# A decoder layer on one core: every engine's order written by hand from the third chunk of the input projection to the end of the attention

## The chip, the cores and the metric

The kernel runs on one core of a Trainium2 chip. Its time is the device time of one execution in microseconds (us); several executions of a kernel are taken, and the median stands for it. The core has five engines that work side by side, each through a queue of its own in a fixed order: PE (TensorE, matrix products), DVE (VectorE), ACT (ScalarE), POOL (GpSimd) and SP (SyncE, which here issues nearly all transfers). An instruction that waits holds up everything behind it in its queue, and nothing else.

## The reference

One layer of a decoder for 256 positions with a model width of 2048, batch 1, all in float32:

```python
a_in = _rmsnorm(h, attn_norm_g[i])
proj = a_in @ w_in[i]
z, xbc, dt_raw, q, k, v = jnp.split(proj, [o1, o2, o3, o4, o5], axis=-1)
xbc = jax.nn.silu(_causal_dwconv(xbc, conv_w[i], conv_b[i]))
xs, bm, cm = jnp.split(xbc, [SSM_INNER, SSM_INNER + SSM_GROUPS * SSM_STATE], axis=-1)
dt = jax.nn.softplus(dt_raw.astype(jnp.float32) + dt_bias[i].astype(jnp.float32))
...
y = y + d_skip[i].astype(jnp.float32)[:, None] * xs_h.astype(jnp.float32)
y = y.reshape(b, s, SSM_INNER) * jax.nn.silu(z.astype(jnp.float32))
...
y_att = _swa_sinks(qh, kh, vh, sinks[i])
h = h + jnp.concatenate([y_ssm, y_att], axis=-1) @ w_out[i]
u = _rmsnorm(h, ffn_norm_g[i]) @ w_up[i]
u = _causal_dwconv(u, ffn_conv_w[i], ffn_conv_b[i])
g_ff, u_ff = jnp.split(u, [D_FF], axis=-1)
h = h + (jax.nn.silu(g_ff) * u_ff) @ w_down[i]
gate = jax.nn.sigmoid(_rmsnorm(h, ple_norm_g[i]) @ w_ple_gate[i])
pe = _rmsnorm(p[i] @ w_ple_proj[i], ple_post_g[i])
h = h + gate * pe
```

The state-space part (SSD) has four groups with 8 heads of 64, a state of 128 and two chunks of 128 positions. The attention has 32 query heads and 8 key and value heads of 64, a window of 128 and a sink for each head; queries and keys are normalised for each head and partly rotated.

## The kernel before

**Steps.** All weights pass through PE in 476 steps of one kind. A step takes 512 KB of weights (`KW = 2` tiles of 128 rows by `NC = 512` columns). SP loads them into `w`; ACT casts them to `wh`, a float rounded to PE's fast format; DVE subtracts, `wl = w - wh`; and PE multiplies twelve times, for 2 row tiles, 2 blocks of 128 positions and three products (high by high, L219; weight's low part, L220; activation's low part, L221). The ring of `w` has `WR = 7` buffers, those of `wh` and `wl` have `WB = 4`. A step's twelve products go to a pair of accumulators, of which there are two pairs; a chunk of `w_in` has 8 steps, a part of `w_out` two for each group of 512 inputs and each 512 outputs.

**Stages.** The first two chunks (B and C of the SSD) and the step sizes `dt` come first. Then follow the 176 steps that the change concerns, counted from 0 at the first step of the third chunk: for each of four groups g a chunk for x and one for z (steps 0 to 63, group g ends its x chunk at 16g + 7), `w_out` of group 0 (64 to 71), the first queries (72 to 79), keys, values, two more chunks of queries (to 111), `w_out` of groups 1 and 2 (112 to 127), the last queries (to 135), `w_out` of 3 and 4 (to 151), and of 5, 6 and 7 (to 175; 4 to 7 are the attention's outputs). Steps 176 to 475 are the feed-forward part and the embedding.

**Beside the steps.** For each group, `ssd_x` scales x out of the accumulators (`scaled`, ACT), turns it to channels, convolves it (`conv_tile`: one ACT operation L266 and three DVE operations L268 for each 128 channels), applies silu, and turns it back. `decays` loads the sums of the step sizes (`seg`), masks them on POOL and takes 16 exponentials on ACT (L513); `decays_cb`, `state` and `heads` are the matrix products of the scan. `norm_rope` normalises and rotates queries and keys, `scores` computes a block of 8 or 4 heads and its softmax, and `values` the product with v. Turning a float32 tile takes three engines: a copy that takes the 16-bit halves apart (`half`), a DMA transpose that SP issues (`flip`), and a copy on POOL that puts them together (`together`, L284). The first copy stands on ACT for x, B, C and y (L293, 128x1024, twenty times) and for the probabilities (L800), otherwise on POOL.

**What sets the order.** In this region only PE's order is the order of the program:

```python
order.enter_context(tc.manual_schedule(engines={PE.engine}))
```

For the other engines a scheduler chooses, by its own model of times. `chunk` and `output` are generators that emit a step at a time, and `plan(n, event)` names the step after which a piece is emitted (decays of a group 4 steps after its x chunk's end, `decays_cb` 9, `state` 18, `heads` 20; scores and values by a table). The feed-forward part is left to the scheduler.

Of the kernel before, what the change touches and what calls it, by code (L numbers as in the profile page):

```python
# [30 lines left out]
WR = 7  # L31
# [34 lines left out]
def hybrid_layer(  # L66
# [208 lines left out]
    def transposed(pool, n, put):  # L275

        half = sb(pool, [P, 2, n], "half", U16)
        put(half)
        flip = sb(pool, [P, 2 * n // P, P], "flip", U16)
        nc.sync.dma_start_transpose(flip, half.rearrange("p a n -> p (a n)"))  # L280
        return flip

    def together(dst, flip):
        G.tensor_copy(dst.bitcast(U16).rearrange("p c (t a) -> p c t a", a=2), flip.rearrange("p (a c) t -> p c t a", a=2))  # L284

    def flipped(pool, dst, n, put):

        together(dst, transposed(pool, n, put))

    def to_channels(pool, t):  # L290

        flips = [
            transposed(pool, NC, lambda half: S.copy(half, halves(t[:, b * NC : (b + 1) * NC]))) for b in range(NB)  # L293
        ]
        for b in range(NB):
            together(v3(t, 4)[:, :, b * P : (b + 1) * P], flips[b])

    def convolve(src, dst, cw, ntap, c0):

        for f in range(4):  # L300
            w = cw[:, (c0 + f) * (ntap + 1) : (c0 + f + 1) * (ntap + 1)]
            conv_tile(src[:, f, :], dst[:, f, :], [w[:, j : j + 1] for j in range(ntap)], w[:, ntap : ntap + 1])

# [58 lines left out]
    def scaled(acc, pool):  # L362

        t = sb(pool, [P, NB * NC], "xa")
        for b in range(NB):
            S.activation(out=t[:, b * NC : (b + 1) * NC], in_=acc[b], func=AF.Copy, scale=rx[:, b : b + 1])
        return t
# [27 lines left out]

    held = {}
    cos_t = sin_t = None
    at = {}
    step = [0]

    def chunk(c, then):
        acc = acc_pair()
        n = KT // KW
        for s in range(n):
            products(acc, aT, load_w(w_in[c, s]), s * KW, KW, KT, s == n - 1)
            if s == n - 1:
                then(acc)
            yield

    def output(*groups):  # L410

        ys_ = [held.pop(i) for i in groups]
        total = KG * len(groups)
        for n in range(4):
            acc = acc_pair()
            for s in range(2 * len(groups)):
                yT = ys_[s // 2]
                products(acc, lambda k, b: yT(k % KG, b), load_w(w_out[groups[s // 2] * 2 + s % 2, n]), s * KW, KW, total, s == 2 * len(groups) - 1)
                if s == 2 * len(groups) - 1:
                    add_to_h(acc, n)  # L420
                yield

    def run(part):
        for _ in part:
            if step[0] in at:
                for event in at[step[0]]:
                    event()
            step[0] += 1

    def plan(n, event):  # L430
        at.setdefault(n, []).append(event)


    order = ctx.enter_context(ExitStack())
    order.enter_context(tc.manual_schedule(engines={PE.engine}))
    with tc.tile_pool(name="ssd", bufs=1) as sp, tc.tile_pool(name="ssd2", bufs=2) as sp2, tc.tile_pool(name="dram", bufs=1, space=bass.MemoryType.DRAM) as dp:
        BT = sb(sp, [P, 4, T], "BT")
        CT = sb(sp, [P, 4, T], "CT")
        raw = [scaled(acc, sp2) for acc in (acc_b, acc_c)]
        for c, (t, dst) in enumerate(zip(raw, (BT, CT))):  # L440
            to_channels(sp2, t)
            convolve(v3(t, 4), dst, scw, 4, 16 + 4 * c)
            S.activation(out=dst, in_=dst, func=AF.Silu)

        dt = sb(sp, [P, 64], "dt")
        dt4 = dt.rearrange("p (g c h) -> p g c h", g=4, c=NB)
        adt = sb(sp, [P, 64], "adt")
        adt4 = adt.rearrange("p (g c h) -> p g c h", g=4, c=NB)
        acs = sb(sp, [P, 64], "acs")
        eacs = sb(sp, [P, 64], "eacs")  # L450
        nacs = sb(sp, [P, 64], "nacs")
        scr = dp.tile([64, P], F32, tag="scr", name="scr")

        def steps_dt():
            tr = tr_tile()
            for b in range(NB):
                PE.matmul(tr[:, b * 32 : (b + 1) * 32], lhsT=dtT[:, b * P : (b + 1) * P], rhs=sel, start=True, stop=True)
            u = sb(sp, [P, 4, NB, 8], "dt_u")
            for b in range(NB):
                V.scalar_tensor_tensor(  # L460
                    out=u[:, :, b, :], in0=v3(tr[:, b * 32 : (b + 1) * 32], 4), scalar=rx[:, b : b + 1], in1=v3(dtb, 4), op0=ALU.mult, op1=ALU.add
                )
            u = u.rearrange("p g c h -> p (g c h)")
            e = sb(sp, [P, 64], "dt_e")
            e1 = sb(sp, [P, 64], "dt_e1")
            l1 = sb(sp, [P, 64], "dt_l1")
            V.scalar_tensor_tensor(out=e, in0=u, scalar=-1.0, in1=u, op0=ALU.mult, op1=ALU.min)
# [543 lines left out]
```

## Time and profile before

| | |
|---|---|
| median of 3 runs | 1451.29 us (1448.86 to 1456.82) |
| the profiled execution, its time | 1453.72 us |
| the profiled execution, its span | 1452.0 us |
| PE's mean granted clock | 0.989 |
| DMA, mean | 207 GB/s, 299.95 MB |

One execution was recorded by the hardware profiler. The page's first part gives each engine's busy time, its share of the span and the number of its instructions. A group of instructions is told by its line, engine and operation, `out<-in`, the shape, the count, the busy time, the mean of one in ns, and the idle time of the engine just before them with what ended it (the releaser). A row of the waits reads: what waited, for what, us in total, times, longest. A row of the timeline has the start, the length, the engine and line, the operation and its count, and in brackets how long the engine was idle before it and what released it. A row on windows has the stretch and its length, each engine's busy time with the number of its instructions, PE's granted clock, DMA's share and its rate.

### The profile page before, as it was taken

The page shows a single profiled execution, that of the slowest core. Times are in us where ns is not written, and L with a number is a line of the kernel's source. Part 1 is how long each engine was busy: PE and PEld are TensorE (multiplying, and loading weights), DVE is VectorE, ACT ScalarE, POOL GpSimd, SP SyncE. Part 2 cuts the span into 40 slices and gives each one's busy share as a digit, 9 for nine tenths or more (in the row PEclk, how much of TensorE's full clock was granted, in tenths as well). Part 3 has the DMA queues.
Part 4 walks back from the last instruction along what each step waited for, and adds up shares of the span by engine and source line. Part 5 has one row for each costly group of instructions (what it writes and reads, how often), then busy time and mean ns, then how long its engine had stood idle before and what let it go on. Part 6 is the DMA issues. An engine that isn't in the chain of part 4 may idle for free.

```text
span 1452.0 us, 17980 instructions
## 1 busy us (share of the span) xinstructions
PE 1421.6 (98%) x6404; PEld 1161.6 (80%) x6404; DVE 979.6 (67%) x1209; ACT 831.1 (57%) x1156; POOL 344.5 (24%) x270
## 2 busy tenths in 40 slices
PE   9999999899899899999999999999999999999998
PEld 6878878788687687888888888888888888888886
DVE  6677758656486878666676746665675576476854
ACT  6785866755465746455565545544553554455643
POOL 0112422405574241001433201411320231120000
PEclk9999999999899999999999999999999999999999
DMA  9867769667587786668878768867876877776671
GB/s 339 267 191 218 220 179 256 171 176 217 145 209 193 199 225 171 208 188 226 223 206 227 205 190 228 211 210 204 211 214 198 219 211 208 206 207 187 213 222 66
DMA packets 193034, 299.95 MB, mean 207 GB/s; under 512 B 122608, under 2 KB 125488, under 8 KB 192560
## 3 DMA queue, kind: packets, MB, share of 16 engines
q1 hardware_dynamic: 192512, 298.33, 72.4%
q8 instruction: 50, 0.82, 0.2%
q10 hardware_dynamic: 432, 0.48, 0.1%
q14 instruction: 40, 0.33, 0.1%
HBM read 268.32 MB, written 2.13 MB: 186 GB/s over the span
## 4 chain that ended last, share of the span: by engine, by line
PE 67%; DVE 0%; issue 0%; ACT 0%; DVEq 0%
PE acc L219 22%; PE acc L220 22%; PE acc L221 22%; PE tr L814 1%; PE tr L252 0%; PE sc L777 0%; DVE sg L941 0%; DVE den L796 0%; DVE wl L193 0%; DVE sg L942 0%; DVE yl L193 0%; DVE h L372 0%; ACT s L792 0%; ACT sg L940 0%; DVEq L1007 0%
## 5 line engine op out<-in xcount | busy, mean ns | idle before, releaser
L193 DVE TENSOR_TENSOR wl<-w,wh 128x1024 fp32r<-128x1024 f32 (+1 forms) x493 | 637.1, 1298 | 412.4 <-ACT wh L192 411.2
L192 ACT CAST wh<-w 128x1024 fp32r<-128x1024 f32 (+1 forms) x493 | 514.4, 1049 | 489.5 <-PE acc L221 460.7
L219 PE MATMUL acc<-wh,ah 128*128 128x512 f32 x1280 | 504.9, 395 | 6.4 <-ACT wh L192 6.4
L220 PE MATMUL acc<-wl,ah 128*128 128x512 f32 x1280 | 501.7, 392 | 5.3 <-DVE wl L193 5.3
L221 PE MATMUL acc<-wh,al 128*128 128x512 f32 x1280 | 501.0, 391 | 0.0
L219 PEld LDWEIGHTS acc<-wh,ah 128*128 128x128 f32 x1280 | 241.9, 189 | 61.3 <-ACT wh L192 7.9
L220 PEld LDWEIGHTS acc<-wl,ah 128*128 128x128 f32 x1280 | 242.0, 189 | 58.5 <-DVE wl L193 6.8
L221 PEld LDWEIGHTS acc<-wh,al 128*128 128x128 f32 x1280 | 242.0, 189 | 50.6
L220 PE MATMUL acc<-wl,gh 128*128 128x512 f32 x352 | 137.0, 389 | 0.0
L221 PE MATMUL acc<-wh,gl 128*128 128x512 f32 x352 | 137.0, 389 | 0.0
L219 PE MATMUL acc<-wh,gh 128*128 128x512 f32 x352 | 136.4, 389 | 0.0
L891 POOL COPY half<-u 128x1024 uint16<-128x1024 uint16 x44 | 60.1, 1376 | 266.0 <-ACT u L889 266.0
L219 PE MATMUL acc<-wh,yh 128*128 128x512 f32 x256 | 102.3, 400 | 5.0 <-ACT z L571 5.0
L220 PE MATMUL acc<-wl,yh 128*128 128x512 f32 x256 | 100.8, 394 | 0.0
L221 PE MATMUL acc<-wh,yl 128*128 128x512 f32 x256 | 100.5, 393 | 0.0
L894 POOL COPY uc<-flip 128x1024 uint16<-128x1024 uint16 x44 | 54.2, 1232 | 175.9 <-DMA flip<-half 175.9
L220 PEld LDWEIGHTS acc<-wl,gh 128*128 128x128 f32 x352 | 66.1, 188 | 13.7
L221 PEld LDWEIGHTS acc<-wh,gl 128*128 128x128 f32 x352 | 66.1, 188 | 13.7
L219 PEld LDWEIGHTS acc<-wh,gh 128*128 128x128 f32 x352 | 66.1, 188 | 13.6
L268 DVE SCALAR_TENSOR_TENSOR cv<-uc,fcw,cv 128x254 f32<-128x254 f32 (+1 forms) x176 | 73.1, 476 | 1.7 <-ACT cv L266 1.7
L219 PEld LDWEIGHTS acc<-wh,yh 128*128 128x128 f32 x256 | 48.6, 190 | 18.5 <-ACT z L571 5.2
L372 DVE TENSOR_TENSOR h<-h,acc 128x512 f32<-128x512 f32 x96 | 62.2, 679 | 1.1 <-PE acc L221 1.1
(227 smaller groups left out, 1194.5 us busy)
## 6 DMA issues: line engine op xcount, KB each, us to landing
w<-in_w_up_dram SPq DMA_DIRECT2D x176, 512.0 KB, 4.2
w<-in_w_in_dram SPq DMA_DIRECT2D x126, 512.0 KB, 4.3
w<-in_w_down_dram SPq DMA_DIRECT2D x88, 512.0 KB, 4.2
w<-in_w_out_dram SPq DMA_DIRECT2D x64, 512.0 KB, 4.4
w<-in_w_pg_dram SPq DMA_DIRECT2D x32, 512.0 KB, 4.2
seg<-scr SPq DMA_DIRECT2D x8, 512.0 KB, 4.9
xt<-in_xT_dram SPq DMA_DIRECT2D x16, 128.0 KB, 6.4
h<-in_x_dram SPq DMA_DIRECT2D x2, 1024.0 KB, 8.5
```

What stands on the lines that cost most here:

```text
L192: S.copy(hi, src)
L193: V.tensor_tensor(out=lo, in0=src, in1=hi.bitcast(F32), op=ALU.subtract)
L219: PE.matmul(acc[b], lhsT=hi, rhs=wh[:, i, :], start=(k == 0), stop=False)
L220: PE.matmul(acc[b], lhsT=hi, rhs=wl[:, i, :], start=False, stop=False)
L221: PE.matmul(acc[b], lhsT=lo, rhs=wh[:, i, :], start=False, stop=(k == total - 1))
L268: V.scalar_tensor_tensor(out=dst[:, s:], in0=ps[:, : T - s], scalar=taps[n - 1 - s], in1=dst[:, s:], op0=ALU.mult, op1=ALU.add)
L372: V.tensor_tensor(out=hs, in0=hs, in1=acc[b], op=ALU.add)
L814: PE.matmul(v3(o[e * HD : (e + 1) * HD, kv * 2 * P : (kv + 1) * 2 * P], 2), lhsT=v[kb][:, vs], rhs=pT[e][:, :, kb, :], start=(kb == 0), st ...
L891: G.tensor_copy(half.rearrange("p (a n) -> p a n", a=2), u_.bitcast(U16).rearrange("p (n a) -> p a n", a=2))
L894: G.tensor_copy(uc[:, :, b * P : (b + 1) * P].bitcast(U16).rearrange("p f (t a) -> p f t a", a=2), flip.rearrange("p (a f) t -> p f t a", ...
```

## The change

From step 0 to step 175 `manual_schedule()` now holds for all engines: every queue has the order of the program. The program is a list of 176 steps, and `run` works through it. In iteration n SP gets the loads up to step n + 8 and ACT the cast of step n + 3 (`ahead`), PE the products of step n, then every chain that is due gets its next piece (`wake`), and last DVE gets the low part of step n + 3 (`low`). A chain is a generator; `yield 5` lets it sleep for five steps. The SSD's `state`, `heads` and the rest of a group are one chain now, `ssd_x`; `add_to_h` is a chain that runs one step after the last product; `rotary`, which computes cosines and sines in some fifty small DVE operations, runs in nine pieces from step 34. The first scores stand two steps later.

Beside the order: `WR` is 6. The twenty copies L293 on ACT are ten copies twice as wide on POOL, and two transposes of 1024 columns are one of 2048. All `half` and `flip` tiles share a pool, `mid`, with two buffers of each; most tiles of the SSD have one buffer instead of two. Table loads on ACT are 17 instead of 22.

```diff
-WR = 7
+WR = 6
...
     def to_channels(pool, t):
-        flips = [
-            transposed(pool, NC, lambda half: S.copy(half, halves(t[:, b * NC : (b + 1) * NC]))) for b in range(NB)
-        ]
+        half = half_tile(pool)
+        G.tensor_copy(half, halves(t))
+        flip = turn(pool, half)
+        yield 5
...
+    def spawn(chain, delay=1):
+        sleepers.setdefault(now[0] + delay, []).append(chain)
+
+    def wake():
+        for chain in sleepers.pop(now[0], []):
+            n = next(chain, 0)
+            if n:
+                spawn(chain, n)
...
+    def ahead(steps):
+        for k in range(len(loaded), min(now[0] + WR + WB - 1, len(steps))):
+            loaded[k] = sb(wp, [P, KW, NC], "w", bufs=WR)
+            nc.sync.dma_start(loaded[k].rearrange("p a b -> p (a b)"), steps[k][0])
+        lows = []
+        for k in range(len(ready), min(now[0] + WB, len(steps))):
+            ready[k] = sb(wp, [P, KW, NC], "wh", F32R), sb(wp, [P, KW, NC], "wl", F32R)
+            S.copy(ready[k][0], loaded[k])
+            lows.append(k)
+        return lows
...
+    def run(steps, until):
+        while now[0] < until:
+            lows = ahead(steps)
+            steps[now[0]][1](ready[now[0]])
+            wake()
+            low(lows)
+            now[0] += 1
...
-    order.enter_context(tc.manual_schedule(engines={PE.engine}))
+    order.enter_context(tc.manual_schedule())
+    mid = mix.enter_context(tc.tile_pool(name="mid", bufs=2))
...
+        yield 1
+        for c in range(NB):
+            for h in range(8):
+                i = heads_[c].start + h
+                S.activation(out=seg[c][:, h, :], in_=seg[c][:, h, :], func=AF.Exp, bias=nacs[:, i : i + 1])
+                if c and h == 3:
+                    yield 1
+            if not c:
+                yield 1
+        yield 2
...
+    low(ahead(steps))
+    scaled(acc_b, raw_b)
+    scaled(acc_c, raw_c)
+    spawn(steps_dt(), 0)
+    spawn(b_or_c(raw_b, BT, 16), 0)
+    spawn(b_or_c(raw_c, CT, 20), 4)
+    spawn(rotary(), 34)
...
             p = s.rearrange("p h w -> p (h w)")
-            flipped(ap_, p.rearrange("p (c t) -> p c t", t=P), 2 * m * W, lambda half: S.copy(half, halves(p)))
+            half = half_tile(mid)
+            S.copy(half, halves(p))
+            flip = turn(mid, half)
+            yield 4
+            together(p.rearrange("p (c t) -> p c t", t=P), flip)
...
-        for j, first, value in ((0, (30, 33, 36), 50), (1, (43, 46, 51), 65), (2, (58, 61, 66), 79), (3, (75, 77, 80), 93)):
+        for j, first, value, wait in ((0, (32, 36, 39), 49, 8), (1, (44, 48, 52), 62, 1), (2, (56, 60, 65), 75, 6), (3, (74, 77, 80), 90, 1)):
```

What this makes of the queues is shown at three places. The first is ACT at the start of the region, before the change: casts of the weights (L192), the scaling of B and C out of the accumulators (L366), and their copies (L293).

```order
L192 CAST wh_632<-w_631 128x1024
L192 CAST wh_650<-w_649 128x1024
L192 CAST wh_668<-w_667 128x1024
L366 ACTIVATE xa_563<-acc_29_147,rx_145 128x512
L366 ACTIVATE xa_563<-acc_30_148,rx_145 128x512
L293 COPY half_569<-xa_563 128x1024
L366 ACTIVATE xa_566<-acc_31_149,rx_145 128x512
L293 COPY half_573<-xa_563 128x1024
```

And ACT at the same place now, where casts are L465 and the scaling is L367.

```order
L465 CAST wh_589<-w_571 128x1024
L465 CAST wh_592<-w_573 128x1024
L465 CAST wh_595<-w_575 128x1024
L465 CAST wh_598<-w_577 128x1024
L367 ACTIVATE xa_563<-acc_29_147,rx_145 128x512
L367 ACTIVATE xa_563<-acc_30_148,rx_145 128x512
L367 ACTIVATE xc_564<-acc_31_149,rx_145 128x512
L367 ACTIVATE xc_564<-acc_32_150,rx_145 128x512
```

The cast of step 3 has come ahead of the scaling, and the copies are gone from ACT.

The second is ACT about step 14, in group 0, before: the exponential of `dec` (L507), the convolution of x (L266), the 16 exponentials of `seg` (L513) and the casts.

```order
L507 ACT_TABLE_LOAD
L507 ACTIVATE dec_949<-dec_949 128x8
L192 CAST wh_1037<-w_1036 128x1024
L266 ACTIVATE xc_810<-xa_797,scw_133 128x256 x4
L513 ACTIVATE seg_947<-seg_947,nacs_627 128x128 x8
L513 ACTIVATE seg_963<-seg_963,nacs_627 128x128 x8
L192 CAST wh_1055<-w_1054 128x1024
L192 CAST wh_1082<-w_1081 128x1024
```

Now the same place (dec at L562, C's silu at L497, `seg` at L571); the casts are those of steps 16, 17, 18 and 19.

```order
L562 ACT_TABLE_LOAD
L562 ACTIVATE dec_928<-dec_928 128x8
L497 ACT_TABLE_LOAD
L497 ACTIVATE CT_562<-CT_562 128x1024
L465 CAST wh_941<-w_807 128x1024
L571 ACT_TABLE_LOAD
L571 ACTIVATE seg_176_872<-seg_176_872,nacs_569 128x128 x8
L465 CAST wh_969<-w_835 128x1024
L266 ACTIVATE xc_984<-xa_826,scw_133 128x256 x2
L571 ACTIVATE seg_177_873<-seg_177_873,nacs_569 128x128 x4
L465 CAST wh_1000<-w_855 128x1024
L266 ACTIVATE xc_984<-xa_826,scw_133 128x256 x2
```

The exponentials stand in three pieces with casts between, and C's silu with its table has come between `dec` and the cast of step 16.

The third is DVE about step 153, where the softmax of two blocks of scores meets `w_out` of the first attention outputs, before: the scores' mask (L781), the maximum (L788), the sums (L796 to L798), the additions to h (L372) and low parts (L193).

```order
L796 TENSOR_TENSOR den_4764<-den_4764,es_4769 128x4
L193 TENSOR_TENSOR yl_1016_4819<-tr_4827,yh_1015_4818 128x4x128
L797 RECIPROCAL den_4764<-den_4764 128x4
L798 TENSOR_TENSOR s_1002_4754<-s_1002_4754,den_4764 128x1024
L193 TENSOR_TENSOR wl_4948<-w_4946,wh_4947 128x1024
L781 TENSOR_TENSOR s_1024_4858<-sc_4859,band_120 128x1024
L372 TENSOR_TENSOR h_1_83<-h_1_83,acc_1019_4838 128x512
L372 TENSOR_TENSOR h_2_84<-h_2_84,acc_1020_4839 128x512
L788 TENSOR_REDUCE nm_4865<-s_1024_4858 128x4
L193 TENSOR_TENSOR wl_4966<-w_4964,wh_4965 128x1024
```

Now (sums L908 to L910, mask L891, maximum L898, the step's low part L471):

```order
L193 TENSOR_TENSOR yl_1011_4837<-tr_4664,yh_1010_4836 128x4x128
L908 TENSOR_TENSOR den_4785<-den_4785,es_4783 128x4
L909 RECIPROCAL den_4785<-den_4785 128x4
L910 TENSOR_TENSOR s_992_4756<-s_992_4756,den_4785 128x1024
L891 TENSOR_TENSOR s_1012_4845<-sc_4811,band_120 128x1024
L898 TENSOR_REDUCE nm_4847<-s_1012_4845 128x4
L471 TENSOR_TENSOR wl_4822<-w_4678,wh_4821 128x1024
L372 TENSOR_TENSOR h_1_83<-h_1_83,acc_1004_4797 128x512
L372 TENSOR_TENSOR h_2_84<-h_2_84,acc_1005_4798 128x512
```

The sums of one block, the mask and the maximum of the next now stand in one piece, and the additions to h behind it and behind the low part.

More of the change, by code (lines that the diff above doesn't have):

```diff
@@ new lines, in hybrid_layer, with chunk, step, products_of @@
+    sleepers = {}
+    now = [0]
+    def spawn(chain, delay=1):
[5 more added lines that the diff above has]
+                spawn(chain, n)
+    def chunk(c, then):
+        n = KT // KW
+        acc = []
+        def step(s):
+            def products_of(w):
+                if s == 0:
+                    acc.extend(acc_pair())
+                products(acc, aT, w, s * KW, KW, KT, s == n - 1)
+                if s == n - 1:
+                    then(acc)
+            return products_of
+        return [(w_in[c, s], step(s)) for s in range(n)]
```

588 lines of the change are left out of this document (312 added, 276 removed).

## The prediction, made before the changed kernel had run

> **What bounds the kernel now.** I read the page first, then the waits of PE, then windows of the span, and last the timeline at the places that the windows point to.
>
> ```profile
> span 1452.0 us, 17980 instructions
> PE 1421.6 (98%) x6404; PEld 1161.6 (80%) x6404; DVE 979.6 (67%) x1209; ACT 831.1 (57%) x1156; POOL 344.5 (24%) x270
> PE sc L777 <- POOL kT L284: 6.7, 1, 6.7
> PE acc L219 <- ACT wh L192: 6.4, 3, 2.4
> PE acc L220 <- DVE wl L193: 5.3, 4, 3.1
> PE acc L219 <- ACT z L571: 5.0, 1, 5.0
> ```
>
> PE is busy for 98% of the span, and nothing here changes its matmuls. So the change can only win PE's waits and what they bring. The last four rows (us in total, times, longest) are nearly all of these waits: 23.4 us. The windows say where they lie (length, then busy time and count for PE, PEld, DVE, ACT and POOL, PE's clock, DMA share, GB/s):
>
> ```profile
> 54.24:625.70 571.46, 548.12 (x2534) 441.83 (x2533) 413.51 (x523) 364.46 (x586) 189.61 (x155) 0.97 0.72 199
> 625.70:1443.00 817.30, 817.30 (x3627) 677.02 (x3626) 526.63 (x586) 428.74 (x519) 152.14 (x103) 1.00 0.73 205
> 700.00:800.00 100.00, 100.00 (x443) 82.81 (x442) 67.08 (x80) 57.69 (x70) 31.78 (x20) 1.00 0.80 218
> 99.33:111.69 12.36, 9.23 (x30) 6.96 (x29) 8.49 (x15) 12.27 (x24) 2.02 (x2) 0.73 0.40 134
> 207.55:218.51 10.96, 7.98 (x30) 6.17 (x29) 3.07 (x4) 10.90 (x19) 3.82 (x4) 0.84 0.28 73
> 262.13:275.73 13.60, 8.60 (x30) 6.80 (x29) 6.74 (x8) 13.12 (x22) 4.98 (x5) 0.75 0.47 111
> 376.38:392.51 16.13, 9.45 (x41) 7.46 (x40) 6.67 (x6) 3.62 (x4) 7.60 (x5) 0.68 0.79 170
> 464.56:481.01 16.45, 10.90 (x38) 7.74 (x36) 10.90 (x12) 13.34 (x19) 7.50 (x4) 0.90 0.68 166
> ```
>
> The first row is the stretch whose order is rewritten, steps 0 to 175; the second is the rest, where PE never waits and runs at full clock. The third gives the price of a step: 443 matmuls in 100 us are 0.226 us each, so a step of twelve takes 2.71 us. The last five rows hold steps 16-17, 49-50, 65-66, 102-103 and 127-129: 11 steps, which at that price are 29.8 us, in 69.5 us. The counts add up to 169, 37 more than the steps' 132; these are 128 columns wide or less where a step's matmuls have 512, for which I allow 0.08 us each, 3 us. So **36.7 us** are lost at five places: about 6.5, 5.0, 7.6, 9.4 and 8.3. Only 23.4 of them are idle; the other 13.3 are work at a lower clock behind the gaps, 0.57 us for each idle one. With all of it gone the profiled execution (1453.7 us) would take 1417.0: the floor of everything below.
>
> ACT is busy for 12.27 of 12.36, 10.90 of 10.96 and 13.12 of 13.60 us in the first three places: there a cast that PE needs stands behind other work on ACT. The fourth is one wait for the turned keys on POOL. The fifth and the first are waits inside an engine's queue:
>
> ```profile
> 464.54 1.90 ACT L800 COPY half<-s 128x2048 uint16<-128x2048 uint16 x1 [8.14 <-DMA flip<-half]
> 95.85 0.21 ACT L507 ACTIVATE dec<-dec 128x8 f32<-128x8 f32 x1 [2.83 <-DVE dec L506]
> 95.97 1.04 ACT L192 CAST wh<-w 128x1024 fp32r<-128x1024 f32 x1
> 96.91 2.07 ACT L266 ACTIVATE xc<-xa,scw 128x256 f32<-128x256 f32 x4
> 98.89 4.78 ACT L513 ACTIVATE seg<-seg,nacs 128x128 f32<-128x128 f32 x16
> 104.65 0.58 PE L219 MATMUL acc<-wh,ah 128*128 128x512 f32 x1 [2.45 <-ACT wh L192]
> 106.51 0.63 PE L221 MATMUL acc<-wh,al 128*128 128x512 f32 x1
> ```
>
> At 464.54 ACT had stood for 8.14 us on a copy that waited for a buffer, with casts behind it. At 95.85 it had waited 2.83 us, and then 2.07 of convolution and 4.78 of exponentials ran ahead of the next casts; PE then stood 2.45 us, and its matmuls took 0.63 us behind it.
>
> **The change, part by part.** *The groups' chains.* The sixteen exponentials now run as 8, cast, 4, cast, 4, and the convolution in pairs of two, so at most 2.4 us (half of 4.78) stand between two casts. A cast starts when PE has left the buffer, three steps ahead: 8.1 us, less 1.04 for itself, are 7.1 us of slack. The twenty ACT copies L293 go to POOL, and table loads fall from 22 to 17. For groups 1 to 3 the pieces of one step (1.04 + 1.04 + 1.2) come to little over a step, so ACT falls behind by less than the slack: steps 49-50 and 65-66 lose nothing, a gain of 12.6. Bounds: 0 to 12.6; I take all, since those windows are full on ACT and it is exactly ACT that is relieved.
>
> *Group 0* has C's silu and its table besides. From `dec` in step 12 to the casts' end in step 13 ACT has 1.5 (table, exponential), 2.3 (table, silu), 1.04 (cast) and 3.7 (table, eight exponentials): 8.5 us in two steps of 5.4, hence 3.1 late. In step 14 a cast and two convolutions add 2.1; then DVE does six additions, and only behind them the low part that PE needs at step 17, 8.1 us after step 14 began.
>
> ```profile
> 95.89 2.14 POOL L508 TENSOR_SCALAR_AFFINE_SELECT seg<-seg 128x1024 f32<-128x1024 f32 x2 [6.05 <-DVE dec L506]
> 97.04 2.08 DVE L193 TENSOR_TENSOR wl<-w,wh 128x1024 fp32r<-128x1024 f32 x1 [1.22 <-ACT wh L192]
> 99.04 4.80 DVE L268 SCALAR_TENSOR_TENSOR xc<-xa,scw,xc 128x255 f32<-128x255 f32 x12
> 104.63 2.36 DVE L193 TENSOR_TENSOR wl<-w,wh 128x1024 fp32r<-128x1024 f32 x2 [0.79 <-ACT wh L192]
> 105.57 1.28 ACT L571 ACT_TABLE_LOAD   x1
> 107.45 1.05 ACT L540 ACTIVATE xc<-xc 128x1024 f32<-128x1024 f32 x1
> ```
>
> 3.1 + 2.1 + 2.4 (half of 4.80) + 1.2 are 8.8, 0.7 too late, and a wait of `dec` for its data as before (2.83) comes on top: 3.5 idle, and 2 to 3 at half clock. That is about what this place loses now, so I keep its **6.5**. Bounds 0 (the data come in time) to 10.
>
> *The start.* Before the first product ACT now makes four casts, not three, ahead of the scaling that frees PE's accumulators.
>
> ```profile
> 50.55 1.05 ACT L192 CAST wh<-w 128x1024 fp32r<-128x1024 f32 x1 [1.67 <-PE acc L338]
> 51.51 1.26 ACT L366 ACTIVATE xa<-acc,rx 128x512 f32<-128x512 f32 x2
> ```
>
> The fourth cast's buffer comes free one step after the third's, at 50.55 + 2.72 = 53.3; cast and first scaling end at 53.3 + 1.05 + 0.63 = 55.0, where PE now starts at 54.24. **+1.0** (0 to 1.5).
>
> *The keys.* Now both key transposes stand late, and PE waits 6.7:
>
> ```profile
> 376.58 5.12 SPq L280 DMA_TRANSPOSE flip<-half  x1
> 382.88 5.05 SPq L280 DMA_TRANSPOSE flip<-half  x1
> 376.70 3.09 POOL L752 COPY half<-qkr 128x1024 uint16<-128x1024 uint16 x2
> 383.77 2.11 POOL L284 COPY kT<-flip 128x2048 uint16<-128x2048 uint16 x1 [3.98 <-DMA flip<-half]
> w<-in_w_in_dram SPq DMA_DIRECT2D x126, 512.0 KB, 4.3
> ```
>
> In the new order the keys' copies stand in steps 91 and 92 and their turning back in 97 and 98; the first scores stand at 104 instead of 102. The chain of copy 3.1, issue 5.1, landing 2.1 (381.70 to 383.77) and copy 2.1 fits twice into twelve steps: the 9.4 go. But both transposes hold up SP's weight loads: a load is issued eight steps ahead of its products, five ahead of its cast, 13.6 us, of which it takes 4.3; 9.3 remain, and two transposes of 5.1 fill 10.2. **+1.0** (0 to 5) at step 101.
>
> *The attention.* A block of probabilities goes to values in 16 steps; from its copy to the values stand five, 13.6 us.
>
> ```profile
> L284 POOL COPY s<-flip 128x2048 uint16<-128x2048 uint16 x12 | 28.4, 2368 | 73.7 <-DMA flip<-half 54.8 <-PE acc L221 18.9
> L781 DVE TENSOR_TENSOR s<-sc,band 128x1024 f32<-128x1024 f32 x12 | 14.6, 1216 | 6.5 <-PE sc L777 6.5
> L788 DVE TENSOR_REDUCE nm<-s 128x4 f32<-128x1024 f32 x8 | 9.7, 1210 | 0.1
> L798 DVE TENSOR_TENSOR s<-s,den 128x1024 f32<-128x1024 f32 x12 | 16.1, 1340 | 0.2
> L372 DVE TENSOR_TENSOR h<-h,acc 128x512 f32<-128x512 f32 x46 | 29.9, 677 | 0.0
> ```
>
> Copy 1.9, issue 5.1, landing 2.1 and turning back 2.4 are 11.5, so ACT and DVE may be 2.1 late. In the steps where two blocks meet DVE has 1.2 (low part) + 1.22 + 1.21 + 1.34, and a carry of additions or a split (1.35): 6.3 in a step of 2.7. I take DVE to be 5 late at the first values (step 121): **+3.0** idle (0 to 7); the later values have longer waits behind them. At output 5 the additions to h now stand one step later, behind such a step: 6.3 + 1.35 against the two steps (5.4) after which PE wants the accumulators, 2.3, and the small ones of the step: **+2.8** (0 to 5). The fifth place (8.3) goes: ACT's copies now stand where their buffers should be free.
>
> *The rest.* One raw weight buffer less takes a step off the loads' lead, everywhere:
>
> ```profile
> L192 ACT CAST wh<-w 128x1024 fp32r<-128x1024 f32 (+1 forms) x493 | 514.4, 1049 | 489.5 <-PE acc L221 460.7
> ```
>
> The casts' idle time ends with PE 460.7 of 489.5 us, not with a load: I cost it at nothing (0 to 3), hidden by loads that wait for buffers. Rotary's small operations on DVE move into steps 34 to 42, between stalls: nothing (0 to 2).
>
> *The clock.* The new gaps, 1.0 + 1.0 + 3.0 + 2.8 = 7.8, bring 0.57 us of slow work each: 4.5 (0 to 7). [...]
>
> **The sum:** 1417.0 + 6.5 + 1.0 + 1.0 + 3.0 + 2.8 + 4.5 = 1435.8 us against the profiled 1453.7, 17.9 less. The median of the runs (1451.29) lies 2.4 below that execution; from it, 17.9 less is 1433.4: I predict **1433.5**.
>
> **The rivals.** *A, nearly all waits go:* the terms of the attention and the keys are zero, the start and half of group 0 remain: 1417.0 + 1.0 + 3.3 + 0.6 = 1422, by the median 1419.5. For it: each of my new terms is a lateness of 0.7 to 3 us against slacks worked out from mean durations.
>
> *B, POOL's new copies hold up DVE:* ten copies 128x2048 at some 2.2 us come to POOL. Above, the low part at 97.04 took 2.08 us beside POOL's work on `seg`; two undisturbed took 2.36. If each copy costs the low part 0.9, and half-clock work follows (0.57), ten are 14: 1435.8 + 14 = 1450, by the median 1447.5. For it: the 2.08. Against: a low part has slack, and 0.9 matters only where it is used up. [...]
>
> *C, slower:* in a fixed order a copy that waits for one of the two buffers stands ahead of the casts, as at 464.54, where one wait of 8.14 cost 8.3. The scores' twelve copies, the queries' and keys' ten and the groups' fourteen now share two `half` and two `flip` buffers. From three such places on, 25 us, the gain is gone by more than 0.5%; with four it is 1435.8 + 33 = 1469, by the median 1466.5. Against: most copies have five steps between, and a chain of 11.5 us fits.
>
> *D, it does nothing that counts:* PE's waits only move to the next piece (group 0 shows how), 1449 to 1454. I count it with B.
>
> **How the numbers follow.** Forecast 0.52 (1427 to 1441), A 0.20 (1417 to 1427), B and D 0.17 (1441 to 1455), C 0.11. The range that leaves out C and A's last few: 1418 to 1453. A measurement of this kernel can tell 0.5%, 7.3 us, from no change: faster than 1444 are the forecast, A and a little of B, 0.73; within, 0.16; slower than 1458.5, 0.11.
>
> **What would show it.** Right: PE's waits on ACT near steps 49 and 65 and on kT absent; a first gap of about 1 us at the first product of the third chunk; a gap of 2 to 5 us at step 17; one of a few us at the first values. Wrong: casts whose idle time ends with a transpose or with a `w` load; PE gaps in 625 to 1443, where there are none now (the seventh buffer); low parts of 2 us in most steps.

## The result and the profile after

The changed kernel takes 1460.58 us (median of 14 runs, 1459.29 to 1465.48); the kernel before took 1452.28 us beside it (14 runs). The ratio is 1.0059 with a 95% interval of 1.0047 to 1.0071: slower by 8.3 us, where 17.9 less had been forecast. The profiled execution took 1459.82 us, 6.1 more than the one profiled before the change; of these 6.1, 4.0 lie in the 176 steps, 1.4 ahead of them and 0.7 behind.

The page's first part of the changed kernel, then its waits of PE (us in total, times, longest):

```profile
span 1458.1 us, 17885 instructions
PE 1420.3 (97%) x6404; PEld 1158.6 (79%) x6404; DVE 1006.5 (69%) x1209; ACT 806.2 (55%) x1131; POOL 365.8 (25%) x276
PE acc L220 <- DVE wl L471: 16.0, 9, 4.1
PE acc L219 <- ACT z L597: 5.3, 1, 5.3
PE tr L932 <- POOL s L284: 4.3, 2, 2.5
PE tr L252 <- DVE h L372: 2.2, 1, 2.2
PE acc L219 <- DVE h L372: 1.7, 1, 1.7
PE acc L219 <- ACT xa L367: 0.8, 1, 0.8
```

The wait for kT is gone and ACT does 25 us less (831.1 before, 806.2 now). But PE's wait for the low parts has gone from 5.3 to 16.0 us in nine places, its wait for z is 5.3 where it was 5.0, and four small waits are new. DVE does the same 1209 instructions in 27 us more. The windows of the rewritten steps and of the rest:

```profile
55.61:631.11 575.50, 545.85 (x2525) 437.61 (x2526) 436.62 (x569) 341.17 (x561) 212.10 (x163) 0.99 0.66 198
631.11:1449.89 818.78, 818.78 (x3637) 678.84 (x3637) 534.70 (x588) 429.76 (x523) 151.13 (x102) 1.00 0.73 205
```

The rest still has no wait (818.78 us against 817.30 in a stretch cut a little otherwise). The rewritten steps take 575.50 instead of 571.46 us, and step 0 starts at 55.61 instead of 54.24. So the question is asked in these 176 steps. For each place I took the time from one step's first matmul to the next step's, less 2.72 us a step and less the other matmuls in it (at what they cost where nothing waits); that is what the place loses, idle time and slow work together. The forecast's terms stand beside it, and the last column is the best of the experiments, e14:

| steps | before | forecast | changed | e14 |
|---|---|---|---|---|
| 0 | 0 | 1.0 | 0.8 | 0.8 |
| 11 to 14 | 0 | 0 | 3.3 | 4.3 |
| 16 to 18 | 6.5 | 6.5 | 6.3 | 0.4 |
| 34 | 0.1 | 0 | 1.7 | 1.7 |
| 37 | 0 | 0 | 5.0 | 0 |
| 49 to 50 | 5.1 | 0 | 3.7 | 1.7 |
| 65 to 66 | 7.7 | 0 | 8.0 | 1.7 |
| 71 to 72 | 0 | 0 | 0.3 | 2.7 |
| 101 to 103 | 9.5 | 1.0 | 0 | 0 |
| 118 to 122 | 0 | 3.0 | 2.3 | 1.9 |
| 127 to 129 | 8.1 | 0 | 0.1 | 0.1 |
| 132 | 0 | 0 | 2.0 | 0 |
| 147 to 148 | 0 | 0 | 4.6 | 0.3 |
| 155 to 158 | 0 | 2.8 | 2.2 | 0.7 |
| 175 | 0 | 0 | 2.3 | 2.3 |
| slow work behind new gaps | | 4.5 | (in the rows) | (in the rows) |
| sum | 37.0 | 18.8 | 42.6 | 18.6 |

The two wins in the attention came as forecast, 17.5 us. They were given back at places where the sum had zeros. The two sums differ by 23.8 us, and the profiled execution missed the forecast for it, 1435.8, by 24.0: the table holds nearly the whole miss.

### The profile page after: what moved, and what is told of

It is laid out like the page before. It is cut to its first block, busy times and chain, and to the rows that moved or that the text cites. A ratio compares the mean times of both kernels' runs of the same rounds, so it can differ in the third digit from the quotient of the medians.

```text
span 1458.1 us, 17885 instructions
## 1 busy us (share of the span) xinstructions
PE 1420.3 (97%) x6404; PEld 1158.6 (79%) x6404; DVE 1006.5 (69%) x1209; ACT 806.2 (55%) x1131; POOL 365.8 (25%) x276
## 4 chain that ended last, share of the span: by engine, by line
PE 80%; DVE 8%; ACT 4%; issue 3%; DMA 2%; POOL 2%; SPq 0%; DVEq 0%; POOLq 0%; ACTq 0%
PE acc L219 25%; PE acc L220 25%; PE acc L221 25%; DVE wl L471 3%; DMA flip<-half 1%; ACT wh L465 1%; PE acc L339 1%; PE acc L340 1%; DVE xc L268 1%; PE acc L338 1%; PE ms L643 1%; ACT seg L571 1%; POOL s L284 1%; DMA seg<-scr 1%; ACT s L906 1%
## 5 line engine op out<-in xcount | busy, mean ns | idle before, releaser
L193 DVE TENSOR_TENSOR wl<-w,wh 128x1024 fp32r<-128x1024 f32 (+1 forms) x317 | 416.7, 1317 | 279.8 <-ACT wh L192 279.2
L192 ACT CAST wh<-w 128x1024 fp32r<-128x1024 f32 (+1 forms) x317 | 332.4, 1048 | 358.1 <-PE acc L221 341.2
L471 DVE TENSOR_TENSOR wl<-w,wh 128x1024 fp32r<-128x1024 f32 x176 | 237.7, 1357 | 90.9 <-ACT wh L465 90.5
L465 ACT CAST wh<-w 128x1024 fp32r<-128x1024 f32 x176 | 182.2, 1047 | 168.2 <-PE acc L221 128.9
```

Source lines behind the costliest of these rows:

```text
L192: S.copy(hi, src)
L193: V.tensor_tensor(out=lo, in0=src, in1=hi.bitcast(F32), op=ALU.subtract)
L465: S.copy(ready[k][0], loaded[k])
L471: V.tensor_tensor(out=ready[k][1], in0=loaded[k], in1=ready[k][0].bitcast(F32), op=ALU.subtract)
```

## The experiments

Four theories went into the runs. **1**: each wait has a piece of its own that stands at a bad place, and the places add up. **2**: POOL's new copies hold up DVE. **3**: weights come late, for want of a buffer or behind wide transposes. **4**: the attention's copies and transposes wait for one of two buffers, of the halves or of the flips. All experiments alter the changed kernel. Medians of before, taken beside each set, were 1454.39 (e1 to e4), 1453.66 (e5 to e8), 1454.95 (e9 to e11), 1453.12 (e12) and 1452.92 us (e13 to e15), and ratios are against these. Since before was up to 2.7 us slower in these sets than beside the changed kernel (1452.28), a gain counted from 1460.58 is uncertain by as much, and the ratios are safer.

Each kernel has one trace, and places that an edit doesn't touch differ between traces too. From the changed kernel to e7, all with two flips, 132 loses 0 to 2.0, 147 to 148 loses 2.8 to 6.6, and step 122 nothing or 1.7. The traced executions of e3, e4 and e7 took 3.0 to 4.2 us more than their medians.

### e1: z of group 3 earlier

```diff
-        steps += chunk(3 + 2 * g, lambda acc, g=g: spawn(ssd_z(g, acc), 3))
+        steps += chunk(3 + 2 * g, lambda acc, g=g: spawn(ssd_z(g, acc), 3 if g < 3 else 1))
```

> The z of group 3 is read out of its accumulators one step after its chunk's end instead of three. Theory 1 (each wait of PE has its own badly placed piece; here z stands two steps behind the step that needs its accumulators): PE's wait of 5.3 us at step 66 goes with the slow work behind it, 5 to 7.6 us less than the changed kernel's 1460.6, so 1453 to 1456. Theory 2 (POOL's new copies hold up DVE's low parts everywhere): the low part of step 66 is late by itself and takes the wait's place, under 2 us less.

Measured: 1457.91 us, ratio 1.0027 (1.0014 to 1.0039). The timeline of the changed kernel shows the wait, ACT first, then PE (start, length, in brackets the idle time before and what ended it):

```profile
272.76 1.04 ACT L465 CAST wh<-w 128x1024 fp32r<-128x1024 f32 x1
275.55 1.28 ACT L609 ACT_TABLE_LOAD   x1 [1.76 <-DVE xc L268]
276.85 1.06 ACT L609 ACTIVATE xc<-xc 128x1024 f32<-128x1024 f32 x1
277.81 1.97 ACT L465 CAST wh<-w 128x1024 fp32r<-128x1024 f32 x2
279.69 1.25 ACT L597 ACTIVATE z<-acc,rx 128x512 f32<-128x512 f32 x2
...
280.42 0.79 PE L219 MATMUL acc<-wh,yh 128*128 128x512 f32 x1 [5.28 <-ACT z L597]
```

The two z operations empty the accumulators that PE wants at step 66, and their chain sleeps three steps. After the other groups a chunk of x of eight steps lies between; after group 3 come parts of `w_out` of two steps, and the third step is already PE's. On ACT, silu with a wait for DVE and two casts stood ahead of z. With one step of sleep the wait is 0.7 us and the place loses 1.8 instead of 8.0. Of these 6.3 us some are found again: 1.5 at steps 69 and 71; 147 to 148 loses 1.5 more, which is within its spread. The trace's 176 steps are 3.4 us shorter. Theory 1 has the place, but not the whole amount.

### e2: rotary later

```diff
-    spawn(rotary(), 34)
+    spawn(rotary(), 70)
```

> Rotary's nine pieces start at step 70 instead of 34. Theory 1: the wait at step 37 (3.1 us, with slow work 5.0) goes and that at 34 stays, 4 to 5 us less, 1455.5 to 1456.5. Theory 2: the low part of step 37, which took 2.53 us beside POOL, stays late; under 1.5 us less.

Measured: 1454.36 us, ratio 1.0000 (0.9989 to 1.0011), more than expected. DVE before step 37 in the changed kernel:

```profile
170.90 1.00 DVE L680 CAST posf<-posi 128x2 f32<-128x2 int32 x1
171.94 2.54 DVE L684 TENSOR_SCALAR ang<-posf 128x2 f32<-128x2 f32 x8
...
175.43 1.21 DVE L586 TENSOR_TENSOR seg<-seg,tr 128x1024 f32<-128x1024 f32 x1
176.56 2.53 DVE L471 TENSOR_TENSOR wl<-w,wh 128x1024 fp32r<-128x1024 f32 x1
```

The first of the nine pieces alone has 14 operations and takes from 170.90 to 175.4 us, 4.5 us in a step of 2.7, and the low part that PE waits for stands behind it. Moved away, the loss of 5.0 at 37 is gone, and 49 to 50 fall from 3.7 to 1.7 too. The later pieces (to step 42) seem to get there through a load: in the changed kernel the `dec` of group 2 waits 2.62 us for `seg` (at 207.54), in e2 and e6 it doesn't wait, and in both step 49 loses nothing. The 2.0 at 132 is gone here as well, which nothing in the edit explains.

### e3 and e5: C and seg of group 0

e3, then what e5 adds to it:

```diff
-    spawn(b_or_c(raw_c, CT, 20), 4)
+    spawn(b_or_c(raw_c, CT, 20), 2)
```
```diff
-    spawn(decays(g), 8 + 16 * g + 2)
+    spawn(decays(g), 8 + 16 * g + (2 if g else -1))
...
-        yield 2
+        yield 2 if g else 5
```

> C's chain starts at step 2 instead of 4, so that its turning back on POOL stands ahead of the copy of group 0's x. Theory 1: C's convolution, dec and the exponentials come some 4 us earlier; the losses at steps 13 to 14 (3.3) and 17 (6.0) fall to 3 or less together: 6 to 9 us less, 1451.5 to 1454.5. A rival: dec waits for seg's load then, as in the kernel before (2.83 us), and step 17 stays: 3 us less.

Measured: 1460.56 us, ratio 1.0047 (1.0029 to 1.0065): nothing won by the medians. The loss at 13 to 14 only moved to 11 to 12 (4.0), and 17 kept 5.5. The timeline of the changed kernel, and behind it that of e3, show two different waits at the same place:

```profile
84.15 2.60 POOL L292 COPY half<-xa 128x2048 uint16<-128x2048 uint16 x1 [19.81 <-ACT xa L367]
86.70 3.27 POOL L284 COPY xc<-flip 128x1024 uint16<-128x1024 uint16 x2
90.00 1.09 ACT L266 ACTIVATE CT<-xc,scw 128x256 f32<-128x256 f32 x2 [1.65 <-POOL xc L284]
98.84 0.21 ACT L562 ACTIVATE dec<-dec 128x8 f32<-128x8 f32 x1 [3.57 <-DVE dec L561]
```

```profile
90.70 4.33 SPq L461 DMA_DIRECT2D w<-in_w_in_dram  x2
95.12 0.86 SPq L558 DMA_DIRECT2D seg<-scr  x2
100.86 0.17 DVE L561 TENSOR_TENSOR dec<-seg,acs 128x8 f32<-128x8 f32 x1 [3.95 <-DMA seg<-scr]
```

In the changed kernel POOL had been idle for 19.81 us ahead of x's copy, and C's turning back stood behind it; so C's convolution came late, and `dec` stood behind that on DVE. With C early, `dec` waited for `seg`: SP issued that load only at 95.12, when two weight loads ahead of it (90.70, 4.33 us) had their buffers.

> C's chain starts at step 2, and group 0's seg is loaded at step 7 instead of 10 (dec still at 12). With C early alone, dec waited 3.95 us for seg, whose load SP had issued behind weight loads that waited for a buffer. Theory 1 (the chain C, dec, exponentials sets steps 11 to 17): both losses, 3.3 and 6.0, go but for 1 to 3: 6 to 8 us less than the changed kernel's 1460.6, 1452.5 to 1454.5. A rival: at step 17 ACT has too much work in any case (table loads, silu, exponentials), and half of the 6.0 stays: 3 to 5 us less.

Measured: 1455.90 us, ratio 1.0022 (1.0007 to 1.0037). Step 17 loses nothing now (6.0 before), while 11 still loses 4.1. The amount is that of the rival, its reason is not: what stays is at 11, where C's convolution takes 4.18 us for six operations on DVE beside POOL's copy of x (so in e3's trace too, at 85.32, the copy at 84.86 for 1.90 us; 2.95 in the changed kernel, at 90.64, where the copy was over at 86.75).

### e4: seven buffers again

```diff
-WR = 6
+WR = 7
```

> The seventh raw weight buffer back. Theory 1: only the first two chunks' loads gain, the 1.37 us by which step 0 starts later: 1 to 2 us less, 1458.6 to 1459.6. Theory 3 (weights come late because a buffer is missing and wide transposes hold SP): PE's waits for low parts behind late loads go, 6 us or more less.

Measured: 1460.69 us, ratio 1.0045 (1.0027 to 1.0062): the buffer costs nothing that these runs can tell, and theory 3 falls in this form. Step 0 started at 58.24 us here, so the seventh buffer doesn't bring the earlier start back.

### e6: the copies on ACT again

```diff
-        G.tensor_copy(half, halves(t))
+        S.copy(half, halves(t))
```

> The ten wide copies of x, B, C and y stand on ACT again, all else as in the changed kernel. Theory 2 (POOL's copies hold DVE up): DVE's busy time falls by 10 us or more of the 27 that it has gained, the low parts at steps 34 and 50 come in time, and the kernel takes 4 to 6 us less. Theory 1: ten copies of 1.9 us come back to ACT, which is over its steps' length at each group's end; the waits at steps 17, 49 to 50 and 65 to 66 grow by 1 to 2 us each: 3 to 6 us more.

Measured: 1459.00 us, ratio 1.0038 (1.0023 to 1.0052), between the two. DVE's busy time fell by 7.8 us (1006.5 to 998.7), not by 10 or more; the losses at 34 and 49 to 50 fell from 5.4 together to 0.7; but 10 to 14 rose from 3.3 to 5.0 and 37 from 5.0 to 6.9. How a copy of POOL reaches PE at step 34, in the changed kernel (DVE, POOL, PE):

```profile
157.76 2.95 DVE L268 SCALAR_TENSOR_TENSOR xc<-xa,scw,xc 128x255 f32<-128x255 f32 x6 [1.57 <-ACT xc L266]
162.10 4.25 DVE L268 SCALAR_TENSOR_TENSOR xc<-xa,scw,xc 128x255 f32<-128x255 f32 x6 [0.25 <-ACT xc L266]
166.27 2.36 DVE L471 TENSOR_TENSOR wl<-w,wh 128x1024 fp32r<-128x1024 f32 x2
...
160.69 2.91 POOL L292 COPY half<-y 128x2048 uint16<-128x2048 uint16 x1 [3.93 <-ACT y L661]
...
167.54 0.51 PE L220 MATMUL acc<-wl,ah 128*128 128x512 f32 x1 [1.28 <-DVE wl L471]
```

The same six operations take 2.95 us by themselves and 4.25 beside the copy of y, which runs until 163.60; the low part follows them, and PE waits 1.28 for it. In e6, with the copy on ACT, both sixes take 2.95 or 2.96 and PE doesn't wait there. This is theory 2, true at a few places and for 1.3 us each, not everywhere. Of the 27 us that DVE gained, e6 accounts for 7.8; where the rest comes from isn't shown.

### e7 and e13: three half buffers, three flip buffers

e7, and by itself e13:

```diff
-        return sb(pool, [P, 2, NB * NC], "half", U16).rearrange("p a n -> p (a n)")[:, : 2 * n].rearrange("p (a n) -> p a n", a=2)
+        return sb(pool, [P, 2, NB * NC], "half", U16, bufs=3).rearrange("p a n -> p (a n)")[:, : 2 * n].rearrange("p (a n) -> p a n", a=2)
```
```diff
-        flip = sb(pool, [P, 2 * NC * NB // P, P], "flip", U16)
+        flip = sb(pool, [P, 2 * NC * NB // P, P], "flip", U16, bufs=3)
```

> Three buffers for the halves instead of two, flips still two. Theory 4 (in the attention a copy waits for one of two half buffers and holds up the casts behind it, 1.7 us before step 121 and 2.5 us before step 147): the losses at 121, 132 and 147 to 148 (2.2, 2.0, 4.6) go mostly: 5 to 8 us less. Rival: SP waits there for POOL's copies of the queries, which DVE's work holds up, and the weights behind it come late; buffers change nothing, within 1.5 us.

Measured: 1462.39 us, ratio 1.0061 (1.0041 to 1.0082). The losses at 121, 132 and 147 stay: it isn't the halves. Ahead of step 147 in the changed kernel, POOL, SP, ACT, and then PE's wait in that step:

```profile
524.54 3.19 POOL L284 COPY s<-flip 128x2048 uint16<-128x2048 uint16 x1
537.84 2.12 POOL L284 COPY s<-flip 128x2048 uint16<-128x2048 uint16 x1 [5.90 <-DMA flip<-half]
...
527.76 1.24 SPq L279 DMA_TRANSPOSE flip<-half  x1
529.10 1.00 SPq L461 DMA_DIRECT2D w<-in_w_out_dram  x2
530.20 5.46 SPq L279 DMA_TRANSPOSE flip<-half  x1
...
534.17 1.05 ACT L465 CAST wh<-w 128x1024 fp32r<-128x1024 f32 x1 [6.91 <-DMA w<-in_w_out_dram]
...
540.01 1.08 PE L932 MATMUL tr<-s,v 128*64 128x256 f32 x8 [2.49 <-POOL s L284]
```

A cast waited 6.91 us for a weight load. SP had issued it only at 529.10, behind a transpose that started at 527.76, when POOL's copy out of a flip had ended. PE's own wait, 2.49 us, isn't for these weights but for the turned probabilities: their transpose stands next in SP's queue, at 530.20, and POOL's copy of them starts at 537.84, after 5.90 us of waiting for it.

> The changed kernel with three flip buffers instead of two, halves still two. In the changed kernel SP began the transpose of the queries before step 147 at 527.76, just as POOL's copy out of a flip ended (524.54, 3.19 us), and the weight load behind it came so late that a cast waited 6.9 us. Theory 4 in its other form (flips, not halves): the loss at 147 to 148 (4.6) goes, and that at 132 (2.0) perhaps: 4 to 6 us less than 1460.6, 1454.5 to 1456.5. Rival: SP waits for the half, which POOL makes late in any case: within 1.5 us.

Measured: 1457.73 us, ratio 1.0027 (1.0012 to 1.0041). The same transpose, in the trace of e13:

```profile
523.82 1.04 POOL L830 COPY half<-qkr 128x1024 uint16<-128x1024 uint16 x1
524.79 3.17 POOL L284 COPY s<-flip 128x2048 uint16<-128x2048 uint16 x1
...
524.88 1.23 SPq L279 DMA_TRANSPOSE flip<-half  x1
526.21 1.00 SPq L461 DMA_DIRECT2D w<-in_w_out_dram  x2
527.99 4.43 SPq L279 DMA_TRANSPOSE flip<-half  x1
```

It starts as soon as its half is written, 3 us earlier, and the weights and the transpose of the probabilities behind it 3 and 2 us earlier. 147 to 148 lose 0.3 instead of 4.6, and 121 loses 1.3 instead of 2.2; 132 stays at 2.0. The 176 steps are 4.2 us shorter, the median 2.9. Theory 4 holds for the flips, at 147 as the rows show and at 121 by its effect: a transpose that waits for a flip holds up what stands behind it in SP's queue, the next transpose and weight loads.

### e8: four placements at once

e1, e2 and e5, and the additions to h in the step of the last product:

```diff
-                    spawn(adding(acc, n))
+                    spawn(adding(acc, n), 0)
```

> Four placements at once: z of group 3 one step after its chunk, rotary from step 70, C and seg of group 0 early, the additions to h in the step of the last product. By theory 1 the places add up: 3.4 and 7.5 us as measured in the traces, 6 to 8 for C and seg, 1.9 for the additions at step 157: 18 to 20 us less than the changed kernel, 1440 to 1443, and faster than the kernel before by over 0.5%. A rival: each wait taken away is found again some steps on, and half of it comes: 1449 to 1452.

Measured: **1439.11 us**, ratio 0.9900 (0.9885 to 0.9915): 21.5 us under the changed kernel, and faster than the kernel before by 14.5. The page and the longest waits of e8:

```profile
PE 1413.6 (98%) x6404; PEld 1154.4 (80%) x6404; DVE 1005.3 (70%) x1209; ACT 803.4 (56%) x1129; POOL 370.1 (26%) x276
PE acc L220 <- DVE wl L471: 6.9, 7, 2.3
PE tr L932 <- POOL s L284: 3.8, 2, 2.0
```

DVE is still 26 us busier than before, with the same instructions, and it hardly matters: what counted was which piece stood ahead of the low part. The places add up: in the traces the 176 steps are 21.1 us shorter, where e1, e2 and e5 had won 3.4, 7.5 and 5.6 and the additions were put at 1.9. Where the 2.7 above these 18.4 come from isn't shown: 132 and 147 to 148 lose 3.3 less there, which is within their spread, and 71 to 72 lose 2.4 more.

### e9 to e12: what is left

e9, against e8, and e10, against e8 too; e11 is both, and e12 has only the second part of e9:

```diff
-    spawn(b_or_c(raw_c, CT, 20), 2)
+    spawn(b_or_c(raw_c, CT, 20), 3)
...
-        yield 1
+        yield 3
         yield from to_channels(mid, y)
```
```diff
-        for j, first, value, wait in ((0, (32, 36, 39), 49, 8), (1, (44, 48, 52), 62, 1), (2, (56, 60, 65), 75, 6), (3, (74, 77, 80), 90, 1)):
+        for j, first, value, wait in ((0, (32, 36, 39), 50, 7), (1, (44, 48, 52), 62, 1), (2, (56, 60, 65), 76, 5), (3, (74, 77, 80), 90, 1)):
```

> e8_placed_again with two copies moved away from DVE's convolutions: C's chain starts at step 3, so its convolution comes a step after POOL's copy of x, and the copy of y comes two steps later, behind the convolution of the next group's x. Theory 2 in its narrow form (a POOL copy costs PE only where it runs beside DVE work that is already last): the losses at 11 (4.2), 34 (1.7) and 50 (1.7) go to under 1 each, 5 to 7 us less than e8's 1439.1, 1432 to 1434. If ACT's work at the group's end is the cause (convolution, exponentials, y's scaling between the casts), 34 and 50 stay, and 11 alone may go: 0 to 4 less.

> e8_placed_again with the first and third values one step later (their splits at the same step as now). If the last turn of the probabilities is simply one step too late for them, the losses at 121 (2.3) and 147 (2.2) go: 3 to 5 us less than e8's 1439.1, 1434 to 1436. Rival: step 147 is late because weights are late (casts waited 6.9 us for loads that SP issued behind a transpose), and only 121 goes: 2 us less.

> e9 and e10 together. If places add up, as theory 1 has it: the sum of both gains, 8 to 12 us less than e8's 1439.1, 1427 to 1431.

Measured: 1440.99 (ratio 0.9906, 0.9883 to 0.9929), 1439.40 (0.9900, 0.9872 to 0.9927) and 1442.84 us (0.9912, 0.9891 to 0.9933). All three missed: nothing is won over e8. The places named did what was expected of them: with y's copy later 34 and 50 fell from 1.7 to 0.4 each, and with the values later 121 and 147 fell from 2.3 and 2.2 to 0.1. But e9's loss at 11 came back at 12 (4.1) and 17 to 18 (2.0), and e10 loses 1.4, 1.8 and 2.9 at 128, 132 and 155 to 156, 4.2 more than e8 there.

> e8_placed_again with only the copy of y two steps later, C's chain at step 2 again. e9's trace had the losses at 34 and 50 down from 1.7 to 0.4 each, and gave it back at 12, 17 and 18, where C's later start worked. If that is the division, 11 stays (4.2), 17 and 18 are small again, and the kernel takes 2 to 3 us less than e8's 1439.1: 1436 to 1437.5. If y's later copy is itself what is found again (at 71, where x's last turn waits, or at 39), within 1 us of e8.

Measured: 1441.43 us, ratio 0.9919 (0.9900 to 0.9938). 34 and 50 stay at 0.4 each, and 71 to 72 lose 4.9 instead of 2.7; with some 0.5 each at 54, 70 and 156 that eats the gain. From e8 on, the wait of a piece that is moved to another step is found again: theory 1 held for the large misplacements and not for waits of 1 to 2 us.

### e14 and e15: flips and the start, on e8

e14 is e8 with e13's three flips. e15 is e8 with the fourth cast behind the scaling:

```diff
+    now[0] = -1
     low(ahead(steps))
+    now[0] = 0
     scaled(acc_b, raw_b)
```

> e8_placed_again with three flip buffers. Theory 4 in its other form: the loss at 147 (2.4 there) goes, others stay: 2 us less than 1439.1, 1436 to 1438. If what is taken away is found again, as in e9 to e12: 1438.5 to 1441.

Measured: **1435.92 us**, ratio 0.9885 (0.9870 to 0.9900), the fastest. 147 loses 0.1 instead of 2.2 and 121 1.2 instead of 2.3; 132 loses nothing instead of 0.9, but it loses nothing in e15 either, with two flips. Here nothing is found again: a buffer takes a wait away and moves no work.

> e8_placed_again with three casts ahead of the scaling at the start, as in the kernel before, and the loads and the low part of step 3 in iteration 0. My term of the start: PE's wait for the scaling (0.8 us at step 0) goes, 0.8 us less, 1438 to 1439. If the order at the start also makes step 0 begin late (54.24 in the kernel before, 54.8 to 58.2 in the experiments), it begins near 54.2 here, and 1.5 to 2 us more are won.

Measured: 1438.20 us, ratio 0.9904 (0.9889 to 0.9919), 0.9 under e8 by the medians and nothing by the ratios. PE's wait for the scaling at step 0 is gone from the trace, and step 0 begins at 55.62 us all the same: the fourth cast makes the wait, and leaving it out doesn't bring the earlier start back.

## Why the prediction was wrong, point by point

- **The floor, the rest and the keys: right.** PE waits for nothing behind step 176, the keys' 9.4 and the 8.3 at 127 to 129 went (0 and 0.1 left). The 1.0 at step 101 didn't come.
- **"Steps 49-50 and 65-66 lose nothing, a gain of 12.6": the step that failed.** They lose 11.7. I had read ACT's full windows as one cause and relieved ACT. But the row of the waits named z, with 5.0 us, and the question was where z stands now: behind the cast and behind a sleep of three steps. e1 shows it. At 49 to 50, and newly at 34, PE's wait was for a low part on DVE, through rotary (e2: 3.7 to 1.7) and through the copy of y beside the convolution (e6, e9: to 0.4 at 50). The two aren't separate amounts: e6 took 49 to 50 to 0.4 with rotary in its place.
- **Rotary "between stalls: nothing (0 to 2)": 5.0 at step 37, and 2.0 at 49 to 50** (e2). I counted its operations as small, and didn't add up its first piece, 4.5 us in one step's queue.
- **Group 0, 6.5: the size right (6.3), the reason half, so partly luck.** The wait of `dec` that I carried over from the trace of before was one for `seg`'s load. In the changed kernel it is one for DVE (3.57 us), because C's turning back stands behind x's copy on POOL, and that also costs 3.3 at 13 to 14, which I had not seen. When it is taken away the load's wait is there again (e3, 3.95). Both gone, step 17 loses nothing (e5), so my work on ACT (8.5 us in two steps) doesn't bind by itself.
- **The start, +1.0: 0.8.** Besides, step 0 begins 1.4 us later in this execution. In the experiments' traces it begins at 54.8 to 58.2, and only one trace of before shows 54.24; neither the seventh buffer (e4) nor three casts (e15) brought 54.24 back. A spread of 3.4 us between kernels of nearly the same start is more than the 1.4, so it isn't shown that the change makes it late at all.
- **The attention, +3.0 and +2.8: 2.3 and 2.2, two of four.** 132 and 147 to 148 lose 6.6 more. I had priced chains by themselves, and not what a transpose that waits for a flip holds up on SP: at 147 the transpose of the probabilities that PE waits for, and weights (e13). It is in the 2.3 at the first values too, of which three flips take 0.9, so that term isn't DVE's lateness alone. The 2.0 at 132 is gone in e14, but in e2 and e15 as well and not in e13, so its cause stays open. At 175 a transposition waits for the additions to h, 2.3, in every experiment; it wasn't tried.
- **The clock, 4.5: too much.** Of the four gaps that it was put on, one didn't come, and none of the others (0.78, 1.82 and 1.70 us, at steps 0, 121 and 157) brought a lower clock in this trace; the gaps at 34, 50 and 121 (1.28, 2.05, 1.82 us) cost 0.4 us beyond themselves each, those of 3.1 us and more 1.9 to 2.7. In all, PE's waits of the list above are 30.3 us and the table's other 12.3 are 0.41 for each, instead of 0.57. How much of it comes differs between executions at one length of the gap (last section).
- **The rivals.** B's mechanism is there, at 34 and 49 to 50 with about 4.7 us of the 42.6, in the convolution ahead of the low part. The 2.95 and 4.25 us above are the measure: at 162.10 the six operations began 1.5 us before the copy ended, at 163.60, and lost 1.3; by what means a copy on POOL slows DVE isn't shown. But B's general price, 14 us for ten copies, isn't there: all ten moved to ACT win 1.6 us by the medians (e6). C, the slower one, named a wait for one of two buffers; e7 and e13 show it for the flips, on SP instead of ACT, at 147 to 148 with 4.3 us and at 121 with 0.9. Most of the rest of the slowness came from neither, but from pieces that I had set at zero: z, rotary and C.

## What to carry to other kernels

In this order, written by hand, what a step cost was set by the pieces that stand ahead of the instruction PE waits for, not by the engine's load. So list, for each wait of the old profile, the instruction that it names, and find that instruction in the new order, with all that is queued ahead of it in its step. Sleeps in fixed steps must be checked against each consumer by itself; z's three steps were right for three groups and cost 6.3 us at the fourth's end. And an order that is off by a few pieces gives back what it wins: the same change with a few numbers altered is 1.0% faster than before instead of 0.6% slower (e8), and 1.15% with one more buffer (e14).

## What the runs showed of the hardware that was not expected

Gaps of PE of the same length brought a lower clock in one execution and not in another. Each of these windows starts with a step's first matmul and holds one gap; the column behind POOL's is PE's clock. First step 37 of the changed kernel, with a gap of 3.13 us, and the same step of e5, with 3.50:

```profile
175.63:183.37 7.74, 4.61 (x13) 3.32 (x12) 7.50 (x15) 1.85 (x3) 2.12 (x1) 0.78 0.61 196
169.68:176.20 6.52, 3.02 (x14) 2.17 (x12) 6.38 (x9) 1.85 (x3) 2.12 (x1) 1.00 0.75 231
```

Step 11 of e8, with a gap of 2.35 us, and of e3, with 2.34; and step 49 of e7, with 1.74:

```profile
87.65:94.61 6.96, 4.62 (x13) 3.35 (x12) 6.75 (x13) 4.38 (x7) 0.00 (x0) 0.75 0.64 158
87.96:93.32 5.36, 3.02 (x14) 2.18 (x12) 5.15 (x11) 3.06 (x5) 0.00 (x0) 1.00 0.73 164
219.16:225.88 6.72, 4.98 (x18) 3.82 (x17) 6.31 (x10) 4.94 (x11) 2.92 (x1) 0.77 0.52 121
```

A gap of 3.50 us left the clock at 1.00, and one of 1.74 took it to 0.77 over the step. The gap of 2.18 or 2.19 us at step 175, which the changed kernel and all fifteen experiments have, had slow matmuls behind it in seven of the sixteen traces, where step 176 took 1.5 to 1.7 us longer; in the changed kernel's the clock was 1.00 behind it (631.11 to 636.00). So between 1.74 and 3.50 us no length decides here, and what does isn't shown. A place in a table of this kind can differ by some 1.7 us between two executions for this alone.

POOL's times differ beside DVE as well: four rotations that took 1.16 us in one place of the attention (438.94), beside a reduction on DVE, took 4.10 in another (518.72), beside low parts and a softmax product. Whether DVE's work makes the difference isn't shown.
